# A tiled matmul with bias and residual: two input tiles loaded ahead of the first residual, one cast moved to VectorE, eight transposes moved one tile down

## The chip, the cores and the metric

The kernel runs on one core of a Trainium2 chip. The metric is the device time of one execution in microseconds (us); lower is better. A core has TensorE (PE; its weight loads are listed as PEld), VectorE (DVE), ScalarE (ACT), GpSimd (POOL) and SyncE (SP), which here only issues transfers. Sixteen DMA engines move data between HBM (the large memory) and SBUF (the core's working memory). PSUM is the memory that TensorE writes its results to. One transfer is split over all sixteen, and each of them reports its own share as landed; the transfer has landed when the last one reports.

## The reference

```python
def setup_inputs():
    batch, m, k, n = 16, 512, 1024, 768
    # x (batch, m, k), weight (k, n), bias (n), residual (batch, m, n), all float32
def reference(x, weight, bias, residual):
    return (np.matmul(x, weight) + bias + residual).astype(np.float32)
```

That is 8192 rows of x: 64 tiles of 128 rows, in 8 groups of 8 tiles. Read are 33.6 MB of x, 3.1 MB of weight and 25.2 MB of residual; written are 25.2 MB.

## The kernel before

Each tile of x is cast to bf16, transposed on TensorE in eight 128x128 pieces, copied from PSUM to SBUF by VectorE, and multiplied with the weight in 16 matmuls. VectorE and GpSimd add bias and residual, and the residual's buffer is stored as the output. All big transfers are issued by SyncE on one queue, so they are served in the order of the program. Cut to what matters:

```python
    # the start of the one DMA queue, in this order
    load_x(0, 0, 2)      # group 0, tiles 0 and 1
    load_x(0, 2, 3)
    load_w(0); load_w(1); load_w(2); load_w(3)
    load_x(0, 3, 4)
    load_x(0, 4, 6)
    load_res(0, 0, 4)    # residual of tiles 0 to 3, 1.5 MB
    load_x(0, 6, 8)      # tiles 6 and 7, 1 MB
    load_x(1, 0, 4)
    load_res(0, 4, 8)
    ...
    def transp(t):
        if t < n_t:
            pt = ring(ps, "pt", t, 2, [P, len(steps), P], BF16)
            for i, (c, e) in enumerate(steps):
                K_(nc.tensor.transpose(out=pt[:, i, :], in_=xb[t][:, c, :, e], identity=ident))
            xt[t] = ring(sb, "xt", t, 4, [P, len(steps), P], BF16)
            K_(nc.vector.tensor_copy(out=xt[t], in_=pt))
    ...
    # prologue: tiles 0 to 2 together, weight chunk by weight chunk
    cast(HEAD)           # tile 3, ScalarE
    cast(HEAD + 1)
    for c in range(n_c):
        for t in range(HEAD):
            mms(t, 2 * c)
            mms(t, 2 * c + 1)
            if c == n_c - 1 and t == 0:
                finish(0)
                pool_add(0)
                transp(HEAD)
    ...
    # main loop: one tile after the other; the next tile's transposes sit inside it
    for t in range(HEAD, n_t):
        cast(t + 2)
        ...                               # loads of group S + 2
            if 1 <= S < n_s - 1:
                store(S - 1)
        if t < n_t - 1:
            for i in range(len(steps)):
                mms(t, i)
                ...
                if i == T_STEP:
                    transp(t + 1)
        ...
        if S == n_s - 1 and j == 0:
            store(S - 1)
        if S == n_s - 1 and j == J // 2:
            store(S, 0, J // 2)
        if S == n_s - 1 and j > J // 2:
            store(S, j - 1, j)
    # the last tile is finished and stored in two pieces, 256 KB and 128 KB
```

Of the kernel before, what the change touches and what calls it, by code (L numbers as in the profile page):

```python
# [12 lines left out]
HEAD = 3  # L13
# [8 lines left out]
def kernel(  # L22
# [14 lines left out]
    n_c = K // (2 * P)  # L37
# [14 lines left out]
    def ring(pool, name, i, n, shape, dt):  # L52
        return pool.tile(shape, dt, name=name, tag=f"{name}{i % n}", bufs=1)
# [8 lines left out]
    def load_x(S, j0=0, j1=J):  # L62
        if S < n_s:
            if j0 == 0:
                x_sb[S] = ring(sb, "x_tile", S, X_BUFS, [P, J, K], FP32)
            K_(nc.sync.dma_start(out=x_sb[S][:, j0:j1, :], in_=x_d[S, :, j0:j1, :]))  # L66

    def load_res(S, j0=0, j1=J):
        if S < n_s:
            if j0 == 0:  # L70
                ro[S] = ring(sb, "ro", S, RO_BUFS, [P, J, N], FP32)
            K_(nc.sync.dma_start(out=ro[S][:, j0:j1, :], in_=res_d[S, :, j0:j1, :]))
# [10 lines left out]
    def cast(t, engine="act"):  # L83
        if t < n_t:
            xb[t] = ring(sb, "xb", t, 4, [P, n_c, P, 2], BF16)
            copy = nc.scalar.copy if engine == "act" else nc.vector.tensor_copy
            K_(copy(  # L87
                out=xb[t].rearrange("p c i e -> p (c i e)"), in_=x_sb[t // J][:, t % J, :]
# [9 lines that stand above are left out]
# [8 lines left out]
    def mms(t, i):  # L106
        if i == 0:
            po[t] = psum_o(t)
        for n0, nl in chunks:
            mm(t, i, n0, nl)  # L110

    def row(t, n0=0, nl=N):
        return ro[t // J][:, t % J, n0:n0 + nl]

    def pool_add(t):
        if 0 <= t < n_t:
            r = row(t)
            K_(nc.gpsimd.tensor_add(out=r, in0=r, in1=tmp[t] if t < EARLY else bias_sb))  # L118

    def finish(t, n0=0, nl=N):  # L120
        if t < 0:
            return
        p = po[t][:, n0:n0 + nl]
        if t < EARLY:
            tmp[t] = ring(sb, "tmp", t, TMP_BUFS, [P, N], FP32)
            K_(nc.vector.tensor_add(out=tmp[t], in0=p, in1=bias_sb))  # L126
        else:
            K_(nc.vector.tensor_add(out=row(t, n0, nl), in0=p, in1=row(t, n0, nl)))  # L128
# [13 lines left out]
    load_w(3)  # L142
    load_x(0, 3, 4)
    load_x(0, 4, 6)
    load_res(0, 0, 4)
    load_x(0, 6, 8)
    load_x(1, 0, 4)
    load_res(0, 4, 8)
    load_x(1, 4, 6)
# [43 lines left out]
    for c in range(n_c):  # L193
        cast_w(c, 0, "act")
        cast_w(c, 1, "dve")
        if c == 0:
            K_(nc.vector.tensor_copy(out=bias_sb, in_=bias_ps))  # L197
    cast(HEAD)
    cast(HEAD + 1)
    for c in range(n_c):  # L200
        for t in range(HEAD):
            mms(t, 2 * c)
            mms(t, 2 * c + 1)
            if c == n_c - 1 and t == 0:
                finish(0)
                pool_add(0)
                transp(HEAD)
    finish(1)
    pool_add(1)
# [34 lines left out]
    t, S = n_t - 1, n_s - 1  # L244
# [36 lines left out]
```

## Time and profile before

| | before |
|---|---|
| median of 6 runs | 211.81 us (211.39 to 212.16) |
| span of the profiled run | 210.1 us |
| TensorE busy | 202.0 us (96%) |
| DMA data queue, share of 16 engines' span | 97.7% |

From the page of the profile of the kernel before: busy time by engine, the DMA busy share in 40 equal slices (tenths), the queue table (packets, MB, share of 16 engines), and the chain of work that ended last, by engine.

```profile
span 210.1 us, 3634 instructions
...
PE 202.0 (96%) x1555; PEld 131.0 (62%) x1555; DVE 104.3 (50%) x138; ACT 69.1 (33%) x69; POOL 115.1 (55%) x71
...
DMA  6999999999999999999999999999999999999984
...
q1 hardware_dynamic: 6192, 87.03, 97.7%
q8 instruction: 12, 0.20, 0.4%
...
PE 85%; DMA 12%; ACT 1%; DVE 0%; SPq 0%; issue 0%; ACTq 0%
```

Two resources are full from start to end, TensorE and the DMA queue. The chain names TensorE. It ends with VectorE's last addition, at 205.49 + 0.43 = 205.92 us (start, length, what); the last stores and the wait for them, up to 210.1 us, are not in it:

```profile
205.49 0.43 DVE ro L128
```

The second queue, with 12 packets of 16 KB, carries instructions; such a transfer is called an instruction fetch below.

The timeline of TensorE in the kernel before (start, length, what, count; in brackets the idle time before it and what ended it):

```profile
16.99 0.62 PE L95 MATMUL pt<-ident,xb 128*128 128x128 bf16 x8 [0.34 <-ACT xb L87]
17.45 2.76 PE L101 MATMUL po<-w_sb,xt 128*128 128x512 bf16 x16
...
27.27 0.62 PE L95 MATMUL pt<-ident,xb 128*128 128x128 bf16 x8 [0.97 <-ACT xb L87]
...
201.39 4.06 PE L101 MATMUL po<-w_sb,xt 128*128 128x512 bf16 x24
```

There are two holes: 0.34 us before tile 3's transposes and 0.97 us before tile 6's. After 27.27 there are no more, and the last matmul ends at 201.39 + 4.06 = 205.45 us. The chain in order of time (start, length, what) says where the larger one came from:

```profile
7.08 19.00 DMA x_tile<-in_x_dram
26.07 0.02 issue
26.09 0.04 ACTq L87
26.13 0.04 issue
26.17 1.05 ACT xb L87
27.23 0.05 issue
27.27 0.62 PE pt L95 x8
```

Tiles 6 and 7 landed at 26.1, behind the residual. The change aims at these two holes.

The sixteen completion records of each transfer, which the trace keeps, show it (an own count from those records, not a view of the profile; us from a start that lies 0.02 us before that of the other views):

```
kernel before                fastest engine  slowest engine  apart  engines over 1.2 us behind
residual of tiles 0 to 3         21.33           23.62        2.29       1
residual of group 3              78.87           81.20        2.33       4
residual of group 5             127.51          129.72        2.22       7
x of group 6                    144.46          146.69        2.23       9
residual of group 6             151.76          155.53        3.77       9
store of group 6                198.13          201.59        3.47       9
first half of group 7's store   201.78          205.24        3.46       9
very last store (128 KB)        207.62          209.00        1.39       1
```

The slowest engine lands share after share at the queue's rate (7.3 us for 3 MB) up to the last one. The fastest engines had run dry. Their 207.62 is, by this reading, about where TensorE's chain alone would have put the end.

### The profile page before, as it was taken

How to read it: one execution, taken by the hardware profiler on the slowest of the kernel's cores; microseconds unless marked ns; L12 is line 12 of the kernel's file. 1: busy time of each engine (PE TensorE's matmuls, PEld its weight loads, DVE VectorE, ACT ScalarE, POOL GpSimd, SP SyncE). 2: the span in 40 equal slices, each digit the busy share in tenths (PEclk: the TensorE clock that was granted, in tenths of full speed). 3: DMA queues.
4: the chain of work that ended last, by engine and by line, in shares of the span. 5: the costliest groups of instructions: out<-in, count | busy, mean ns of one | idle time of the engine just before them, and what ended most of it. 6: DMA issues, size and time to landing. Idle time of an engine off the chain costs nothing.

```text
span 210.1 us, 3634 instructions
## 1 busy us (share of the span) xinstructions
PE 202.0 (96%) x1555; PEld 131.0 (62%) x1555; DVE 104.3 (50%) x138; ACT 69.1 (33%) x69; POOL 115.1 (55%) x71
## 2 busy tenths in 40 slices
PE   7899989999999999999999999999999999999991
PEld 2465656666666666666666666666666666666660
DVE  0645534544554455455445544554554455446551
ACT  2545046330633053232423142330533216231000
POOL 2000483968999805991099802994039930799000
PEclk9999999999999999999999999999999999999999
DMA  6999999999999999999999999999999999999984
GB/s 231 428 422 423 437 417 425 420 433 425 422 480 414 412 440 421 420 451 415 429 438 437 416 423 445 421 443 417 434 426 456 415 413 417 438 445 423 407 359 182
DMA packets 6210, 87.27 MB, mean 415 GB/s; under 512 B 689, under 2 KB 817, under 8 KB 2098
## 3 DMA queue, kind: packets, MB, share of 16 engines
q1 hardware_dynamic: 6192, 87.03, 97.7%
q8 instruction: 12, 0.20, 0.4%
q14 instruction: 4, 0.03, 0.0%
q10 hardware_dynamic: 2, 0.00, 0.0%
HBM read 61.87 MB, written 25.17 MB: 414 GB/s over the span
## 4 chain that ended last, share of the span: by engine, by line
PE 85%; DMA 12%; ACT 1%; DVE 0%; SPq 0%; issue 0%; ACTq 0%
PE po L101 72%; PE pt L95 12%; DMA x_tile<-in_x_dram 12%; ACT xb L87 1%; DVE ro L128 0%; SPq L66 0%; ACTq L87 0%
## 5 line engine op out<-in xcount | busy, mean ns | idle before, releaser
L101 PE MATMUL po<-w_sb,xt 128*128 128x256 bf16 (+1 forms) x1024 | 176.5, 326 | 0.0
L101 PEld LDWEIGHTS <-xt 128*128 128x128 bf16 x1024 | 97.6, 98 | 58.4
L118 POOL TENSOR_TENSOR ro<-ro,bias_sb 128x768 f32<-128x768 f32 x52 | 92.4, 1813 | 50.4 <-DMA ro<-in_residual_dram 40.4
L87 ACT CAST xb<-x_tile 128x1024 bf16<-128x1024 f32 x63 | 64.3, 1045 | 115.3 <-PE pt L95 62.8
L97 DVE COPY xt<-pt 128x1024 bf16<-128x1024 bf16 x64 | 44.2, 692 | 89.2 <-PE pt L95 89.2
L128 DVE TENSOR_TENSOR ro<-po,ro 128x768 f32<-128x768 f32 (+2 forms) x53 | 49.4, 934 | 2.9 <-PE po L101 2.8
L95 PE MATMUL pt<-ident,xb 128*128 128x128 bf16 x512 | 38.9, 219 | 2.2 <-ACT xb L87 1.3
L95 PEld LDWEIGHTS <-xb 128*128 128x128 bf16 x512 | 33.6, 98 | 11.5 <-ACT xb L87 2.4
L118 POOL TENSOR_TENSOR ro<-ro,tmp 128x768 f32<-128x768 f32 x12 | 21.4, 1811 | 28.1 <-DMA ro<-in_residual_dram 21.8
L126 DVE TENSOR_TENSOR tmp<-po,bias_sb 128x768 f32<-128x768 f32 x12 | 11.4, 949 | 1.5 <-PE po L101 1.5
L169 PE MATMUL po<-warm 128*128 128x512 bf16 x15 | 5.3, 516 | 1.2 <-DVE warm L155 1.2
L175 ACT CAST w_sb<-ro 128x768 bf16<-128x768 f32 x4 | 3.3, 832 | 4.0 <-DMA ro<-in_weight_dram 4.0
L169 PEld LDWEIGHTS <-warm 128*128 128x128 bf16 x15 | 1.8, 127 | 3.7 <-issue 2.2
L177 DVE CAST w_sb<-ro 128x768 bf16<-128x768 f32 x4 | 2.2, 555 | 2.5 <-DMA ro<-in_weight_dram 2.5
L87 DVE CAST xb<-x_tile 128x1024 bf16<-128x1024 f32 x1 | 0.7, 694 | 4.6 <-DMA x_tile<-in_x_dram 4.6
L160 ACT ACT_TABLE_LOAD x1 | 1.3, 1283 | 2.0 <-POOL ident masks.py:199 2.0
L189 PE MATMUL po<-tmp 128*128 128x512 f32 (+1 forms) x4 | 1.5, 500 | 0.0
L197 DVE COPY bias_sb<-po 128x768 f32<-128x768 f32 x1 | 1.0, 957 | 0.2 <-PE po L189 0.2
L189 PEld LDWEIGHTS po<-tmp 128*128 128x128 f32 x4 | 0.7, 190 | 0.5 <-issue 0.5
L132 POOL MEMSET tmp<- 128x768 f32 x1 | 0.7, 737 | 0.3 <-POOLq L265 0.3
L155 DVE MEMSET warm<- 128x256 uint32 x1 | 0.3, 272 | 0.9 <-PEq L265 0.9
masks.py:199 POOL TENSOR_SCALAR_AFFINE_SELECT ident<-ident 128x128 bf16<-128x128 bf16 x1 | 0.3, 292 | 0.1
(8 smaller groups left out, 1.0 us busy)
## 6 DMA issues: line engine op xcount, KB each, us to landing
out_dram<-ro SPq DMA_DIRECT2D x7, 3072.0 KB, 23.9
x_tile<-in_x_dram SPq DMA_DIRECT2D x5, 4096.0 KB, 29.3
ro<-in_residual_dram SPq DMA_DIRECT2D x5, 3072.0 KB, 17.7
ro<-in_residual_dram SPq DMA_DIRECT2D x6, 1536.0 KB, 27.0
x_tile<-in_x_dram SPq DMA_DIRECT2D x3, 2048.0 KB, 25.8
x_tile<-in_x_dram SPq DMA_DIRECT2D x5, 1024.0 KB, 19.0
ro<-in_weight_dram SPq DMA_DIRECT2D x4, 768.0 KB, 9.3
out_dram<-ro SPq DMA_DIRECT2D x1, 1536.0 KB, 10.3
```

Of the source, the lines that this page charges most:

```text
L87: K_(copy(out=xb[t].rearrange("p c i e -> p (c i e)"), in_=x_sb[t // J][:, t % J, :]))
L95: K_(nc.tensor.transpose(out=pt[:, i, :], in_=xb[t][:, c, :, e], identity=ident))
L97: K_(nc.vector.tensor_copy(out=xt[t], in_=pt))
L101: K_(nc.tensor.matmul(po[t][:, n0:n0 + nl], lhsT=xt[t][:, i, :], rhs=w_sb[:, c, e, n0:n0 + nl], start=(i == 0), stop=(i == len(steps) - 1),))
L118: K_(nc.gpsimd.tensor_add(out=r, in0=r, in1=tmp[t] if t < EARLY else bias_sb))
L126: K_(nc.vector.tensor_add(out=tmp[t], in0=p, in1=bias_sb))
L128: K_(nc.vector.tensor_add(out=row(t, n0, nl), in0=p, in1=row(t, n0, nl)))
L160: K_(nc.scalar.copy(out=warm_a, in_=warm_a))
L169: K_(nc.tensor.matmul(warm_ps[:, 0:512], lhsT=warm[:, 0:P], rhs=warm, start=True, stop=True))
L175: K_(nc.scalar.copy(out=w_sb[:, c, e, :], in_=w_st[:, c, e, :]))
L177: K_(nc.vector.tensor_copy(out=w_sb[:, c, e, :], in_=w_st[:, c, e, :]))
L189: K_(nc.tensor.matmul(bias_ps[:, n0:n0 + nl], lhsT=ones, rhs=bias_row[:, n0:n0 + nl], start=True, stop=True,))
```

## The change

Its intent is to close both holes. Tiles 6 and 7 are loaded before the first residual. Tile 3 is cast by VectorE (0.69 us a tile) instead of ScalarE (1.05 us), and its transposes come after tile 1's last matmuls instead of tile 0's, so the cast has 0.65 us more time. The whole diff:

```diff
     load_x(0, 4, 6)
+    load_x(0, 6, 8)
     load_res(0, 0, 4)
-    load_x(0, 6, 8)
     load_x(1, 0, 4)
@@
-    cast(HEAD)
+    cast(HEAD, "dve")
     cast(HEAD + 1)
@@
             if c == n_c - 1 and t == 0:
                 finish(0)
                 pool_add(0)
+            if c == n_c - 1 and t == 1:
                 transp(HEAD)
```

## The prediction

> **What bounds the kernel now.** The page calls it a TensorE kernel: PE 96% busy, 85% of the chain that ended last. In the timeline TensorE has two holes after its start: 0.34 us before tile 3's transposes (start 16.99; the ScalarE cast ran 15.89 to 16.93) and 0.97 us before tile 6's (start 27.27; the cast waited for x6,x7, landed about 26.1). From 27.27 on TensorE runs without a gap, 3.05 us per tile, to 205.5.
>
> But the DMA queue is as full: 97.7% of 16 engines' span. The trace's completion records (16 per transfer, one per DMA engine) show the slowest engine never resting. Its 4 MB loads end 9.65 us apart, its 3 MB transfers 7.3 us apart, right to the end: the first half of the last group's stores lands at 205.24, then the 384 KB stores at 206.16, 207.10 and 208.01, and the last two at 208.67 and 209.00, each at the queue's rate. The fastest engine finished the last store at 207.62: that is where the TensorE chain reaches. So I read the end as set by the slowest DMA engine, about 1.4 us behind TensorE. This is the Trainium skill's first case in "Perfetto Trace Analysis", section What "DMA-bound" means: specific DMA engines.
>
> Why that engine lags: it falls 1.55 us behind near 20.7 and again near 151.7 us, when a 16 KB instruction packet runs (12 such packets, 0.20 MB, in the queue table). "Runtime: NRT & Kernel Launch", section Instruction fetch mechanics, says each engine refills in 16 KiB blocks through its own DMA queue; the trace agrees in size. TensorE's instruction count is unchanged, so I expect the same fetches.
>
> **What the change does.** No bytes or matmuls are added or removed. One cast goes from ScalarE (1.05 us) to VectorE (0.69). Eight transposes move behind four matmuls (0.65 us).
> - x6,x7 skip 1.5 MB (3.7 us at the queue's rate): they land near 21 to 22.5, well before tile 6 wants them near 26. The 0.97 us hole closes.
> - Tile 3: VectorE casts from 15.9 to 16.6; the transposes start near 17.1 without a wait. Only four matmuls now stand between them and tile 3's matmuls, and the PSUM copy (about 0.64 us after the first transpose, 0.69 long) ends near 18.5, so a new wait of about 0.25 us appears there.
> - Tile 8's data still lands at 31.0 (same bytes ahead); its cast ends near 32.15, and TensorE will want it near 32.0: 0.1 to 0.2 us lost.
> - The first residual lands near 26.1 instead of 23.6; GpSimd's first additions slip by 2.5 us, but the four tmp buffers absorb that.
> Net: TensorE ends about 1.1 to 1.2 us earlier.
>
> **On the critical path.** If TensorE set the end, the time would be about 210.7. As the slowest DMA engine does, almost none arrives: the last stores wait longer in a queue that drains at the same time.
>
> **Predicted:** 211.8 us, 211.2 to 212.3 eight times in ten. Faster by over 2%: 0.01; within 2%: 0.985; slower: 0.005.
>
> **What would show it.** Right: TensorE's last matmul near 204.3, the last landing still near 209.0 on the slowest engine, longer issue-to-landing for the last stores (now 3.0 us). x6's cast near 21 to 22.5; no hole at 26; a small one near 18.3. Wrong: the last landing moves with TensorE to about 207.9.
>
> **What would make it wrong.** Fetches falling on other engines, or costing less beside 8 KB packets than beside the residual's 12 KB, would move the slowest engine by up to 1.5 us; or that engine has idle time that I don't see, and up to 1.2 us is gained.

## More of the kernel before

The end of the kernel, in windows of time (window, length, busy us of PE, PEld, DVE, ACT and POOL with counts, granted clock, DMA busy share, GB/s), and what SyncE waited for at the very end (total us, times, longest):

```profile
200.00:204.00 4.00, 4.00 (x31) 2.39 (x29) 2.52 (x3) 0.00 (x0) 0.00 (x0) 1.00 0.91 378
204.00:206.00 2.00, 1.45 (x11) 0.86 (x9) 1.12 (x2) 0.00 (x0) 0.00 (x0) 1.00 0.74 298
206.00:208.00 2.00, 0.00 (x0) 0.00 (x0) 0.00 (x0) 0.00 (x0) 0.00 (x0) 1.00 0.68 256
```

```profile
SPq L276 <- DMA out_dram<-ro: 2.7, 1, 2.7
```

The DMA share falls to 0.68 while the kernel still waits for its last store. So most engines are done, and some are not.

## The result

| | before | after |
|---|---|---|
| median of 6 runs | 211.81 us (211.39 to 212.16) | 211.63 us (211.21 to 211.92) |
| ratio | | 0.9991, 95% interval 0.9974 to 1.0007 |
| last matmul ends (profiled run) | 205.45 us | 204.06 us |
| slowest engine's last landing | 209.00 us | 208.89 us |

A ratio is the mean time of one kernel's fast runs over that of the other's in the same rounds, so it is not quite the ratio of the medians. The interval holds 1: no change in time.

The profile of the changed kernel, in the same views. The page:

```profile
span 210.0 us, 3632 instructions
...
PE 202.7 (97%) x1555; PEld 131.7 (63%) x1555; DVE 104.9 (50%) x139; ACT 67.6 (32%) x68; POOL 115.1 (55%) x71
...
q1 hardware_dynamic: 6192, 87.03, 97.7%
q8 instruction: 12, 0.20, 0.4%
...
PE 96%; DVE 1%; issue 0%
```

The timeline of TensorE, and one line each of ScalarE, VectorE and GpSimd:

```profile
17.09 0.61 PE L95 MATMUL pt<-ident,xb 128*128 128x128 bf16 x8
17.54 2.42 PE L101 MATMUL po<-w_sb,xt 128*128 128x512 bf16 x12
...
25.89 0.61 PE L95 MATMUL pt<-ident,xb 128*128 128x128 bf16 x8
...
200.00 4.06 PE L101 MATMUL po<-w_sb,xt 128*128 128x512 bf16 x24
```

```profile
22.28 1.99 ACT L87 CAST xb<-x_tile 128x1024 bf16<-128x1024 f32 x2 [2.15 <-DMA x_tile<-in_x_dram]
...
27.72 0.96 DVE L126 TENSOR_TENSOR tmp<-po,bias_sb 128x768 f32<-128x768 f32 x1 [0.49 <-POOL ro L118]
...
25.88 7.14 POOL L118 TENSOR_TENSOR ro<-ro,tmp 128x768 f32<-128x768 f32 x4 [23.90 <-DMA ro<-in_residual_dram]
```

Neither hole is left. Tiles 6 and 7 are cast from 22.28 on, 3.9 us earlier (it was 26.17), and tile 6's transposes start at 25.89 without a wait. GpSimd starts its first additions at 25.88 instead of 23.74, and VectorE once waits 0.49 us for it, which holds up nobody. TensorE ends 205.45 - 204.06 = 1.39 us earlier, and the chain is now 96% TensorE. Not all of this is the change: in this profiled run VectorE's first cast, which waits for the first x tiles, starts 0.35 us earlier (5.49 instead of 5.84), so an estimate of what the change itself gave is 1.39 - 0.35, about 1.0 us.

The moved transposes leave a small new wait, visible in the chain around 17 to 20 us: the last matmuls of tile 2 (0.65 us) are over before VectorE has copied tile 3 out of PSUM. From tile 3's transposes (17.09) to tile 4's (19.80 in the same timeline) pass 2.71 us, where eight transposes and twelve matmuls take 0.45 + 1.95 us, so the wait is about 0.3 us.

```profile
17.26 0.46 PE pt L95 x8
17.72 0.02 issue
17.74 0.70 DVE xt L97
18.45 0.05 issue
18.49 1.47 PE po L101 x8
```

The end of the kernel in the same windows, and the last wait of SyncE:

```profile
200.00:204.00 4.00, 4.00 (x27) 2.25 (x24) 2.34 (x3) 0.00 (x0) 0.00 (x0) 1.00 0.93 386
204.00:206.00 2.00, 0.07 (x1) 0.00 (x0) 0.42 (x1) 0.00 (x0) 0.00 (x0) 1.00 0.89 352
206.00:208.00 2.00, 0.00 (x0) 0.00 (x0) 0.00 (x0) 0.00 (x0) 0.00 (x0) 1.00 0.39 148
```

```profile
SPq L277 <- DMA out_dram<-ro: 3.7, 1, 3.7
```

Here is the gain: TensorE hands over its last tile 1.39 us earlier, and SyncE then waits 3.7 us for the last store instead of 2.7. The fastest engine lands its share at 206.41 (it was 207.62), the slowest at 208.89 (it was 209.00).

### The profile page after: what moved, and what is told of

Its sections match the earlier page's. It is cut to its first block, busy times and chain, and to the rows that moved or that the text cites. A ratio compares the mean times of both kernels' runs of the same rounds, so it can differ in the third digit from the quotient of the medians.

```text
span 210.0 us, 3632 instructions
## 1 busy us (share of the span) xinstructions
PE 202.7 (97%) x1555; PEld 131.7 (63%) x1555; DVE 104.9 (50%) x139; ACT 67.6 (32%) x68; POOL 115.1 (55%) x71
## 3 DMA queue, kind: packets, MB, share of 16 engines
q1 hardware_dynamic: 6192, 87.03, 97.7%
## 4 chain that ended last, share of the span: by engine, by line
PE 96%; DVE 1%; issue 0%
PE po L101 79%; PE pt L95 14%; PE po L169 3%; PE po L189 1%; DVE xt L97 0%; DVE ro L128 0%; DVE warm L155 0%
## 5 line engine op out<-in xcount | busy, mean ns | idle before, releaser
L87 ACT CAST xb<-x_tile 128x1024 bf16<-128x1024 f32 x62 | 62.8, 1044 | 115.5 <-DMA x_tile<-in_x_dram 54.2
L95 PEld LDWEIGHTS <-xb 128*128 128x128 bf16 x512 | 34.2, 99 | 8.8 <-DVE xb L87 0.7
L169 PE MATMUL po<-warm 128*128 128x512 bf16 x15 | 6.1, 581 | 1.2 <-DVE warm L155 1.2
L87 DVE CAST xb<-x_tile 128x1024 bf16<-128x1024 f32 x2 | 1.4, 693 | 4.9 <-DMA x_tile<-in_x_dram 4.9
```

Of the source, the lines that this page charges most:

```text
L87: K_(copy(out=xb[t].rearrange("p c i e -> p (c i e)"), in_=x_sb[t // J][:, t % J, :]))
L169: K_(nc.tensor.matmul(warm_ps[:, 0:512], lhsT=warm[:, 0:P], rhs=warm, start=True, stop=True))
```

## The experiments

Theories, with names used in the expectations:
- A: the slowest DMA engine sets the end; TensorE alone would be done earlier and has slack.
- B: TensorE sets the end, as the chain of the profile says, and what it gains at the start is lost later.
- C: the total rate of the queue sets the end, and the lag of single engines does not matter.
- The fetch theory, a part of A: the slowest engine is slow because instruction fetches fall on it.

Each kernel was timed in five rounds beside the kernel before on the same chip. The kernel before was at 211.47, 211.48 and 211.36 us in the three jobs. The diffs show the changed calls; where a helper got a new argument for it, that part is left out.

### Taking 3 MB of stores away from the kernel before and from three others

The output of group 2 is then missing; TensorE has the same work. The edit was made to the kernel before, to the changed kernel, and to each half of the change:

```diff
-            if 1 <= S < n_s - 1:
+            if 1 <= S < n_s - 1 and S - 1 != 2:
                 store(S - 1)
```

> The kernel before, without the store of row group 2 (3 MB less to move, output wrong in those rows on purpose; TensorE has the same work). Theory A (the slowest DMA engine sets the end, TensorE is about 1.4 us behind it in slack): the DMA queue is relieved of 7.3 us, so TensorE's chain now sets the end: 211.8 - 1.4 = 210.4 us. Theory B (TensorE sets the end in both kernels, and the time gained at the start is given back later): no change, 211.8 us.

> The changed kernel, without the store of row group 2. Theory A: with the DMA queue out of the way the 1.39 us that TensorE gained (last matmul 205.45 before, 204.06 after) shows in full: 209.0 us, 1.4 us under light_before. Theory B: the gain is given back as in the full kernels, so within 0.3 us of light_before.

> The order of the loads alone, without the store of row group 2. Theory A: TensorE loses the hole before tile 6 only (27.27 - 26.14 = 1.13 us): 209.3 us. Theory B: as light_before.

> The cast on VectorE and the moved transposes alone, without the store of row group 2. Theory A: whatever TensorE saves at tile 3 (0.25 us) it waits again at tile 6, whose data lands at 26.1 as before: no gain, 210.4 us as light_before. Theory B: as light_before too.

| without group 2's store | median us | ratio to the kernel before, 95% interval |
|---|---|---|
| kernel before | 210.16 | 0.9934 (0.9922 to 0.9946) |
| changed kernel | 209.17 | 0.9886 (0.9873 to 0.9899) |
| order of loads alone | 209.27 | 0.9894 (0.9879 to 0.9908) |
| cast and transposes alone | 210.25 | 0.9940 (0.9928 to 0.9951) |

Removing 7.3 us of DMA work bought the kernel before only 211.47 - 210.16 = 1.31 us: by that much TensorE alone would have been done earlier than the queue. With the queue out of the way the change is worth 210.16 - 209.17 = 0.99 us, and the two intervals do not meet. Theory B expected no difference, neither from the missing store nor between the two. SyncE's last wait, in the kernel before and in the changed one without that store, is now the same:

```profile
SPq L276 <- DMA out_dram<-ro: 1.5, 1, 1.5
```

```profile
SPq L277 <- DMA out_dram<-ro: 1.5, 1, 1.5
```

The order of the loads is worth all of it, within 0.1 us; the cast and the transposes alone are worth nothing. The timeline shows why, first without that store in the kernel before, then with the cast and the transposes alone:

```profile
26.67 0.62 PE L95 MATMUL pt<-ident,xb 128*128 128x128 bf16 x8 [0.62 <-ACT xb L87]
```

```profile
27.02 0.62 PE L95 MATMUL pt<-ident,xb 128*128 128x128 bf16 x8 [1.13 <-ACT xb L87]
```

Whatever TensorE saved at tile 3 it waited again at tile 6, whose data came no earlier. The size for the whole change was missed: 0.99 us instead of 1.39. In this job's profiled run of the kernel before, the hole at tile 6 was 0.62 us and not 0.97, so there was less to win; 0.99 agrees with the 1.0 us that are left of 1.39 without the late start of the first profile.

### A little less DMA work, a little more TensorE work

Both start from the changed kernel. One leaves out one tile's store (384 KB, output wrong there), the other does the transposes of four tiles twice.

```diff
             if 1 <= S < n_s - 1:
-                store(S - 1)
+                store(S - 1, 1 if S - 1 == 2 else 0)
```

> The changed kernel, without one tile's store (384 KB of group 2, wrong there on purpose). Theory A (slowest DMA engine sets the end): its share takes 0.92 us, so 211.6 - 0.9 = 210.7 us. Theory B (TensorE sets the end): 211.6 us.

```diff
-                    transp(t + 1)
+                    transp(t + 1, 2 if t in (20, 28, 36, 44) else 1)
```

> The changed kernel with the eight transposes of four tiles done twice (4 x 0.45 = 1.8 us more TensorE work in mid-kernel, result right). Theory A: TensorE has about 2.4 us of slack in the changed kernel (fastest engine's last landing 206.8, slowest 209.25), so no change: 211.6 us. Theory B: 213.4 us.

Without 384 KB the kernel took 210.58 us, ratio 0.9959 (0.9947 to 0.9971). The changed kernel itself was at 0.9991 in its own rounds, which were of another job, so the step is 0.0032, about 0.7 us, where 0.92 was expected; the two intervals together are wide enough for either, but not for zero as theory B has it. With the doubled transposes the last matmul ended at 205.72 us in the profiled run (the slowest of its six, 212.32 us) instead of 204.06, and the kernel took 211.63 us, ratio 1.0013 (0.9997 to 1.0028). The interval meets that of the changed kernel. The 1.8 us that B expected are not there; a few tenths may be. (The landings in this expectation, 206.8 and 209.25, lie about 0.37 us above those given here, 206.41 and 208.89; the slack that it rests on, their distance, is the same.)

### What makes one engine the slowest

The kernel's instructions are 64 bytes each on TensorE by the Trainium skill's account, "Runtime: NRT & Kernel Launch", section Instruction fetch mechanics: blocks of 16 KiB hold 256 instructions. The page of the profile counts 1555 + 1555 = 3110 of them, 12.1 blocks, and 12 packets of 16 KB in the instruction queue, which agrees. In the records above the number of engines that are behind grows with these packets (1, 4, 7, 9), and the distance grows a second time (2.23 to 3.77 us) right after the ninth packet, at 151.7 us. The count is not exact: nine engines are over 1.2 us behind after eight packets, and another queue has four instruction packets of 8 KB. The records don't name the engines, so this needed a test. The first kernel has no transposes and no PSUM copies from tile 8 on and multiplies with old tiles instead (wrong). The second is the same with eight one-column matmuls put in each of those tiles, which brings the instruction count back to the old one.

```diff
     def transp(t):
-        if t < n_t:
+        if t >= J:
+            xt[t] = xt[4 + t % 4] if t < n_t else None
+        elif t < n_t:
```

> The changed kernel without the transposes and PSUM copies of tiles 8 to 63 (it multiplies with the tiles 4 to 7 again; wrong on purpose). TensorE has 56 x 0.45 = 25 us less work and 896 fewer instructions, so 8 or 9 fetches of 16 KB instead of 12. All bytes of data stay. Theory A, with the fetches as the cause of the slowest engine's lag: no engine or at most one is hit twice, so the slowest engine ends up to 1.55 us earlier: 210.1 us if none is, 211.6 if one still is. Theory C (the queue's total bandwidth sets the end, the lag of one engine does not matter): 211.6 us. Theory B: about 187 us.

```diff
             xt[t] = xt[4 + t % 4] if t < n_t else None
+            if t < n_t:
+                pd = ring(ps, "pt", t, 2, [P, 512], FP32)
+                for i in range(len(steps)):
+                    K_(nc.tensor.matmul(pd[:, i:i + 1], lhsT=warm[:, 0:P], rhs=warm[:, 0:1], start=True, stop=True))
```

> The kernel without transposes, with eight one-column matmuls put into each of tiles 8 to 63: the instruction count of TensorE is that of the changed kernel again (1551 weight loads, 1553 matmuls), with no transposes, no PSUM copies and the same wrong output as without them. Fetch theory (a 16 KB instruction packet sets back the DMA engine that it runs on, and the fifth and later ones of a second round make the slowest engine): 12 packets of 16 KB again, four engines hit twice, and the time returns to 211.5 us (211.2 to 211.9). Rival D (it was the transposes and copies themselves, not the fetches, that cost the 1.6 us): it stays at 209.95 us.

Without transposes the kernel took 209.95 us, ratio 0.9929 (0.9917 to 0.9942). The page, with busy times, queues and chain:

```profile
PE 180.7 (87%) x1107; PEld 106.9 (51%) x1107; DVE 71.3 (34%) x83; ACT 64.9 (31%) x68; POOL 114.8 (55%) x71
...
q1 hardware_dynamic: 6192, 87.03, 98.2%
q8 instruction: 8, 0.13, 0.3%
...
DMA 82%; PE 7%; SPq 2%; ACT 1%; POOL 1%; DVE 1%; issue 0%; POOLq 0%; ACTq 0%
```

TensorE was busy 22 us less (180.7 against 202.7 in the changed kernel), and the time fell by only 1.5. Even with TensorE far from full the same bytes take about 210 us, and now the chain names the DMA. With the instructions put back the time was 211.44 us, ratio 0.9999 (0.9985 to 1.0012), and the page has these busy times, queues and chain, with SyncE's last wait under it:

```profile
PE 189.9 (91%) x1555; PEld 117.5 (56%) x1555; DVE 71.3 (34%) x83; ACT 64.9 (31%) x68; POOL 114.9 (55%) x71
...
q1 hardware_dynamic: 6192, 87.03, 97.8%
q8 instruction: 12, 0.20, 0.4%
...
DMA 82%; PE 7%; SPq 2%; ACT 1%; POOL 1%; DVE 1%; issue 0%; POOLq 0%; ACTq 0%
```

```profile
SPq L283 <- DMA out_dram<-ro: 10.7, 1, 10.7
```

This is also the plainest evidence against theory B. The last matmul of this run ends at 196.25 us, 7.8 us before that of the changed kernel, and SyncE then waits 10.7 us for the last store; yet the time is that of the kernel before. Without the instructions the last matmul ends at 196.05 us, so TensorE doesn't explain the 1.5 us between the two runs either. (The granted clock of TensorE was 0.95 to 0.98 in both, against 0.99 to 1.00 in the kernel before; TensorE is not what they wait for.)

So four packets of 16 KB, 64 KB in all beside 87 MB, cost 1.5 us. They do it through the slowest engine, as the completion records of one transfer, the first half of group 7's store, show:

```
                                 fastest  slowest  apart  engines over 2.7 us behind
kernel before                    201.78   205.24   3.46      4
changed kernel                   201.49   205.12   3.63      4
no transposes                    201.28   203.76   2.49      0
no transposes, instructions back 201.43   204.71   3.28      4
```

With 12 packets four engines are 2.7 to 3.7 us behind, with 8 packets none is. The fastest engine hardly moves. In the kernel before and in the changed one the number of such engines is 1, 2, 3 and 4 after the ninth, tenth, eleventh and twelfth packet. This speaks for eight engines that take the fetches in turn, where the ninth to twelfth packet hits four of them again; that the turn is eight long is inferred from these counts, and the run with doubled transposes, also with 12 packets, has five such engines. Theory C, for which such a lag would not matter, does not survive either.

### Moving load between the engines

If some engines are behind, others might carry more. By the Trainium skill, "DMA: Bandwidth & Descriptors", section Why a DMA increments its semaphore by 16 and not by 1, a transfer of 8 partitions runs on the 8 lowest-numbered engines.

```diff
         if S == n_s - 1 and j == 0:
-            store(S - 1)
+            for p0 in range(0, 32, 8):
+                store(S - 1, p0=p0, p1=p0 + 8)
+            store(S - 1, p0=32)
```

> The changed kernel with the store of group 6 split by partitions: four stores of 8 partitions (768 KB in all) and one of 96. All bytes stay. The Trainium skill, DMA: Bandwidth & Descriptors, section on the semaphore increment of 16, says that a transfer with 8 partitions runs on the lowest-numbered 8 of the 16 engines. Theory A: the other 8 engines carry 48 KB less each, 1.83 us at the queue's rate; if those are the ones hit by fetches, the end comes near 209.8 us; if the lowest 8 are the hit ones, near 213.4. Theory C (total bandwidth) or B: 211.6 us.

It took 217.49 us, ratio 1.0284 (1.0269 to 1.0299): 6 us more, which no theory had expected. Each small store had eight completion records from engines, as the page says. But in the records of the packets near the end, 24 KB packets took up to 3.2 us; in the changed kernel they take 0.91 in the median and at most 1.3. A second kernel kept the load of the engines even and split only the partitions:

```diff
-            store(S - 1)
+            store(S - 1, p0=0, p1=P // 2)
+            store(S - 1, p0=P // 2)
```

> The changed kernel with the store of group 6 split into partitions 0 to 63 and 64 to 127 (every DMA engine carries as much as before, result right). It asks why the store split 4 x 8 + 96 cost 6 us. If the uneven load of the engines was the cause: 211.6 us, since here the load is even. If the cause is that a store from part of the partitions reaches only part of the SBUF's ports (Trainium skill, SBUF, State Buffer, section on the DMA port swizzle): each half uses half of the ports and runs at up to half rate, up to 7.3 us more: 214 to 219 us.

It took 218.54 us, ratio 1.0329 (1.0310 to 1.0349), with a correct result. The GB/s line of its page, in slices of 5.4 us:

```profile
GB/s 245 428 421 430 427 410 430 425 439 415 425 446 452 405 427 436 449 421 421 436 421 457 404 436 430 454 399 430 431 437 439 419 422 430 437 363 252 260 336 72
```

Near the end it falls to 252 and 260 GB/s from some 430. That is what the Trainium skill's page "SBUF — State Buffer", section Door 1: The DMA port swizzle, leads one to expect: partitions 0 to 63 reach only 8 of 16 ports, for which it gives about 218 GB/s; a slice here also holds other stores. That the uneven load is not needed for the loss is shown; the ports themselves no run here shows, and how much of the 6 us of the first kernel has the same cause was not measured. So splitting by partitions was a bad tool, and whether load can be moved off the slow engines without that loss stays open. No version was found that beats both kernels.

## Why the prediction was right

- It held that the slowest DMA engine sets the end, 1.4 us behind TensorE's chain. Taking stores away gave 1.31 us and no more, and a TensorE that was done 7.8 us earlier left the time where it was as long as the fetches were the same.
- TensorE's last matmul was expected near 204.3 us; it ended at 204.06. The expected gain of TensorE, 1.1 to 1.2 us, was 1.39 in the profiled run; a loss of 0.1 to 0.2 us at tile 8 did not come: the first x tiles landed 0.35 us earlier in this span (VectorE's first cast at 5.49 instead of 5.84), and tile 8's data with them. That 204.06 lies so near to 204.3 is therefore partly luck. In another job the gain was 0.99 us. The step is right; its size was put a little too high, and it varies from run to run by a few tenths.
- The holes closed as described: tile 6's cast at 22.28 (expected 21 to 22.5), its transposes without a wait, and a new wait near 18.3 us of about 0.3 us (expected 0.25), where the copy ends at 18.4.
- The later residual was absorbed: GpSimd's additions slipped by 2.14 us (expected 2.5), and TensorE waited for none of it.
- The last landing was expected still near 209.0; it came at 208.89. The last wait of SyncE grew from 2.7 to 3.7 us.
- The fetches were expected unchanged, and they were: 12 packets in both. That they cause the lag was only argued then; the pair with 8 and 12 packets shows that it depends on their number.

## What to carry to other kernels

When two resources are full, ask which one finishes last before polishing the other: here the chain of the profile named TensorE in both kernels, while a DMA engine came in last, because that chain ends with the last computation (VectorE's at 205.92 us in the kernel before) and leaves out the stores that are still in the queue. A quick test is to take away some transfers, wrong output and all, and see whether the change then shows in the time. Look at the slowest of the sixteen engines, not at their mean: a 97.7% share hid that the slowest landed its part of a store 3.5 us after the fastest.

## What the Trainium skill lacked or had wrong

- "Runtime: NRT & Kernel Launch", Instruction fetch mechanics, calls the cost of crossing a 16 KiB block "mostly hidden" and doesn't say what a fetch costs the data transfers. In this kernel 12 packets instead of 8 cost 1.5 us (211.44 against 209.95; ratios to the kernel before 0.9999 and 0.9929). The first packet widened the distance between the engines by 1.2 to 1.6 us in the four profiles of the table above.
- "Perfetto Trace Analysis", What "DMA-bound" means, names single DMA engines as a bound and points to each engine's track of busy time, but not to the landings. In the two kernels the chain said 85 and 96% TensorE; the spread of the sixteen completions of one transfer (3.5 us) and a falling DMA share at the end (0.68 while the last store was still out) showed it.
- "DMA: Bandwidth & Descriptors" advises against splitting by partition halves because they serialize on the same engines. Here it also cost rate: 7.2 us with a 3 MB store (218.54 against 211.36 of the kernel before in the same rounds), at 252 to 260 GB/s in the slices where it ran. The port table that foretells this is on the SBUF page.
